# Page tiles laid out on the host for a compressed attention branch, and weights laid out chunk by chunk

## The chip, the cores and the metric

The kernel runs on one core of one Trainium2 chip. The metric is the device time of one launch in microseconds (us), the median of several runs. Laying arrays out anew with numpy before the launch is outside the metric; the arithmetic stays on the chip.

The engines are named as the profile names them: PE is TensorE (PEld its weight loads), DVE is VectorE, ACT is ScalarE, POOL is GpSimd and SP is SyncE, which only issues transfers here.

## The reference

One inference step of a decoder of two layers (width 1024, feed-forward width 2816) over 288 tokens: 256 of a new sequence, and 4 each for 8 running sequences that have 2048 tokens behind them. Each layer is feed-forward, mixer, feed-forward:

```python
for i in range(2):
    x = x + 0.5 * swiglu(rmsnorm(x, norm_ffa[i]), w_ffa_gu[i], w_ffa_down[i])
    h = rmsnorm(x, norm_mix[i])
    x = x + (short_conv_mixer(h) if i == 0 else nsa(h))
    x = x + 0.5 * swiglu(rmsnorm(x, norm_ffb[i]), w_ffb_gu[i], w_ffb_down[i])
y = rmsnorm(x, norm_final)
```

The second mixer is an attention with three branches (compressed, selected, window). The change concerns the compressed branch of the running sequences. Its cache lies in pages of 128 tokens that `page_table` names, 16 pages for each sequence. Every 32 rows of a page become one key and one value:

```python
blk = rows.reshape(B, T // 32, 32, 2, 4, 64) + pe[:, None, None, :]
k = gelu(einsum('bnlkd,lde->bnke', blk[:, :, :, 0], w1k)) @ w2k
v = gelu(einsum('bnlkd,lde->bnke', blk[:, :, :, 1], w1v)) @ w2v
```

Since `pe` is the same for all blocks, the kernel multiplies it by `w1` once and adds the result as a bias `b1`.

## The kernel before, in words

Tokens lie along the free axis: `xT` holds 8 tiles of 128 features by 288 tokens. A product takes a 128x128 piece of weights as the stationary operand. Weights and activations are split in two parts each (`whi`, `wlo`; `xh`, `xl` or `Ah`, `Al`), and three products hi*hi, hi*lo and lo*hi of 288 columns are added up. One unit is such a piece of all 8 feature tiles, 24 products.

Weights come through the class `Weights` (lines 66 to 146). A chunk of up to 1 MB is loaded on SP's queue into one of four `raw` tiles (line 96); it holds two units. `convert` (lines 101 to 123) makes `whi` on ACT (line 116) and `wlo` on DVE or POOL (line 117), two units ahead of the product; when a chunk is used up, the load of the fourth chunk behind it is issued. A chunk is a block of columns of the weight matrix, so each of the 128 partitions reads 8 separate runs of 1 KB (512 bytes in the narrow first chunks).

`begin` (line 329) is the first product of the first layer. It loads `xT` in three parts (line 1454) between the first weight chunks, splits and multiplies as the parts land, and sums the squares. `load_rest` (line 190) sends the convolution state `sT` and the page table `ptb`, the latter to all 128 partitions, on POOL's queue.

In a feed-forward layer (line 431) a gate and an up product give `pg` and `pu`; DVE scales both by `rB`, ACT makes the silu, POOL the gate product `a` (line 456), ACT and DVE split it into `Ah` and `Al`. The 22 pieces go in two halves of 12 and 10, and behind each half comes its part of the down projection. The norm factor `rB` of each stage comes late, from a statistics product `acc<-ss,ones` (line 322).

The compressed branch runs beside all this as a generator, `cmp_side` (line 670). The main program calls `tick` after each unit, and a pacing class lets the generator go on when enough work has passed; `fill.hold` stops it at the end of a stage. Its steps before the change: compute row numbers from the page table on POOL and DVE (`indices`, line 625); load 64 tiles of cached rows with indirect loads on POOL (line 688); turn each on DVE in 32x32 blocks into `rt` (line 694); multiply the bias from `pe` and `W1` on POOL, two long operations (line 707), and reduce it on DVE (line 711); then 16 times a block of 32 small products `acc<-rt,W` over four turned tiles, the second products of the block before (`acc<-Hs,W`, `acc<-W,Hs`), and the gelu on ACT, DVE and POOL (lines 651 to 662), whose result is `Hs`.

Each engine runs its instructions in the order in which the program issues them; the pools of buffers add waits for tiles that are still in use.

Of the kernel before, what the change touches and what calls it, by code (L numbers as in the profile page):

```python
# [10 lines left out]
F32 = mybir.dt.float32  # L11
# [13 lines left out]
NB = 8  # L25
# [13 lines left out]
RAW, SPLIT, RT = 4, 4, 5  # L39
# [25 lines left out]

class Weights:
# [5 lines left out]
    def __init__(self, nc, raw, split, bufs):  # L72
# [8 lines left out]
    def chunk(self, loads, nk, cols):  # L81
        self.chunks.append((loads, nk, cols))
        return len(self.chunks) - 1
# [61 lines left out]
def tile_step(ctx, tc, x_turned, vectors, state_turned, cache_cmp, sel_pages, cache_win, win_pages, page_table,  # L145
              w_ffa_gu, w_ffa_down, w_ffb_gu, w_ffb_down,
              w_conv_in, w_conv_out, w_nsa_in, w_cmp_k1, w_cmp_k2, w_cmp_v1, w_cmp_v2, w_nsa_out,
# [34 lines left out]
    ptb = ffn0.tile([P, P], I32, name="ptb", bufs=1)  # L182
# [27 lines left out]
    W = Weights(nc, raw, split, RAW)  # L210

    def cols_of(w2d, cols, w=256):
        v = w2d.rearrange("(k p) c -> p k c", p=P)
        return [(lambda t: t, v[:, :, cols:cols + w])]
# [4 lines left out]
    def plan_ffn(gu, down, first=False):  # L219
        for f0, f1 in HALVES:  # L220
# [3 lines left out]
            for f, e in zip(cuts, cuts[1:]):  # L224
                g = W.chunk(cols_of(gu, f * P, (e - f) * P), KD, (e - f) * P)
                u = W.chunk(cols_of(gu, FF + f * P, (e - f) * P), KD, (e - f) * P)
# [3 lines left out]
            m = (f1 - f0) // 2  # L230
            dv = down.rearrange("(k p) c -> p k c", p=P)
            for d in range(0, KD, 2):
                cs = [W.chunk([(lambda t: t, dv[:, f0 + i * m:f0 + (i + 1) * m, d * P:d * P + 256])], m, 256)
                      for i in range(2)]
# [4 lines left out]
    def plan_conv():  # L239
        for d in range(0, KD, 2):  # L240
            for part in (1, 2, 0):
                c = W.chunk(cols_of(w_conv_in[0], part * D + d * P), KD, 256)
                for h in range(2):
                    W.unit(c, half(h))
        for d in range(0, KD, 2):
            c = W.chunk(cols_of(w_conv_out[0], d * P), KD, 256)
# [3 lines left out]
    plan_ffn(w_ffa_gu[0], w_ffa_down[0], first=True)  # L250
    plan_conv()
    plan_ffn(w_ffb_gu[0], w_ffb_down[0])
    plan_ffn(w_ffa_gu[1], w_ffa_down[1])

    def plan_nsa():
        v = w_nsa_in[0].rearrange("(k p) c -> p k c", p=P)
        for t in range(6):
            c = W.chunk([(lambda t: t, v[:, :, D + t * 256:D + (t + 1) * 256])], KD, 256)
            for h in range(2):
                W.unit(c, half(h))  # L260
        c = W.chunk([(lambda t: t, v[:, :, D + 6 * 256:N_IN])], KD, 48)
        W.unit(c, lambda v: v)
        for pr in range(2):
            for gp in range(2):
                loads = []
                for kp in range(2):
                    c0 = (2 * pr + kp) * 256 + gp * P
                    loads.append((lambda t, kp=kp: t[:, :, kp * P:(kp + 1) * P], v[:, :, c0:c0 + P]))
                c = W.chunk(loads, KD, 256)
                for gg in range(2):  # L270
                    W.unit(c, lambda v, gg=gg: v.rearrange("p k (kp x) -> p k kp x", kp=2)[:, :, :, gg * HD:(gg + 1) * HD])
        W.attention = len(W.chunks)
        o = w_nsa_out[0].rearrange("(pr kp g d) c -> kp d pr g c", pr=2, kp=2, d=HD)
        for d in range(0, KD, 2):
            loads = []
            for kp in range(2):
                for pr in range(2):
                    loads.append((lambda t, kp=kp, pr=pr: t[kp * HD:(kp + 1) * HD, pr * 4:(pr + 1) * 4],
                                  o[kp, :, pr, :, d * P:d * P + 256]))
            c = W.chunk(loads, KD, 256)  # L280
            for h in range(2):
                W.unit(c, half(h))
        W.stop = W.attention

    plan_nsa()
    plan_ffn(w_ffb_gu[1], w_ffb_down[1])
# [42 lines left out]
    def begin(pg, pu):  # L329
# [26 lines left out]
        sq = []  # L356
        for d in range(0, KD, 3):
            n = min(3, KD - d)
            sq.append(ffn0.tile([P, 3, N], F32, name="rt", bufs=RT)[:, :n])
# [261 lines left out]
    idxc = const.tile([P, 64], I32, name="idxc")  # L621
    pti = const.tile([1, NB * 16], I32, name="pti")
    rows_c = cache_cmp[0].rearrange("n (q l) c k d -> (n q) (l c k d)", l=2)

    def indices():

        pi = ffn0.tile([P, 4], I32, name="pi", bufs=1)
        nc.gpsimd.iota(pi[:, 0:1], pattern=[[0, 1]], base=0, channel_multiplier=1)
        for j, (sh, m) in enumerate(((0, 3), (2, 7), (5, 3))):
            nc.vector.tensor_scalar(pi[:, j + 1:j + 2], pi[:, 0:1], sh, m, op0=OP.logical_shift_right, op1=OP.bitwise_and)  # L630
        pf = ffn0.tile([P, 4], F32, name="pf", bufs=1)
        nc.vector.tensor_copy(pf, pi)
        off = ffn0.tile([P, 4], F32, name="offc", bufs=1)
        nc.vector.scalar_tensor_tensor(off[:, 0:1], pf[:, 1:2], 4.0, pf[:, 3:4], op0=OP.mult, op1=OP.add)
        nc.vector.tensor_scalar(off[:, 0:1], off[:, 0:1], 4.0, None, op0=OP.mult)
        for i in range(1, 4):
            nc.vector.tensor_scalar(off[:, i:i + 1], off[:, 0:1], float(i), None, op0=OP.add)
        pj = ffn0.tile([P, 8], I32, name="pj", bufs=1)
        nc.gpsimd.iota(pj, pattern=[[1, 8]], base=0, channel_multiplier=0)
        hot = ffn0.tile([P, 8], F32, name="hot", bufs=1)  # L640
        nc.vector.tensor_scalar(hot, pj, pf[:, 2:3], None, op0=OP.is_equal)
        pt = ffn0.tile([P, 16, 8], F32, name="pt", bufs=1)
# [874 lines left out]
```

## Time and profile before

| | us |
|---|---|
| median of 3 runs | 1301.99 (1301.74 to 1303.49) |
| profiled execution | 1301.96 |
| its span, first to last instruction | 1300.1 |

| engine | busy us | share | instructions |
|---|---|---|---|
| PE | 1253.6 | 96% | 10679 |
| DVE | 805.6 | 62% | 1476 |
| ACT | 584.1 | 45% | 1050 |
| POOL | 310.0 | 24% | 317 |

The granted TensorE clock is at its full level in nearly all of the span. The transfers move 262 MB, 202 GB/s on average. Products overlap, so that each shows about 0.3 us although one starts every 0.13 us; a busy share of PE therefore tells that no gap was long, not how dense the products are. The stages in order of time: the first feed-forward layer to about 245 us, the convolution mixer to 366, two feed-forward layers to about 826, the projections of the attention to 914, the attention itself to 1050, and the last feed-forward layer.

### The profile page before, as it was taken

Reading aid. Unit: us, or ns where it says so; the run is one execution under the profiler, and the core shown is the slowest. Engines: PE = TensorE matmul, PEld = TensorE weight load, DVE = VectorE, ACT = ScalarE, POOL = GpSimd, SP = SyncE. Lnnn points to the kernel's source line nnn. Section 1 sums busy time; section 2 is a strip of 40 time slices with the busy share of each in tenths; the row PEclk is TensorE's granted clock in tenths of the full one; section 3 lists DMA queues with packets and bytes.
Section 4 is the critical chain, followed back from the end, with each engine's and each line's share of the span. In section 5 each row is a group of like instructions: output and inputs, shape, how many; then the busy total and the mean of one; then the engine's idle time right before and its main releaser. Section 6 shows DMA issues by size and latency. Waiting matters only on the chain.

```text
span 1300.1 us, 26451 instructions
## 1 busy us (share of the span) xinstructions
PE 1253.6 (96%) x10679; PEld 1198.9 (92%) x10679; DVE 805.6 (62%) x1476; ACT 584.1 (45%) x1050; POOL 310.0 (24%) x317
## 2 busy tenths in 40 slices
PE   8999999899999999999999999999888799999997
PEld 8999999899999999999999999999555489999997
DVE  5766666767677656666765455665566456654553
ACT  5443344433444433345433344543566355433444
POOL 1240322343232312232421021220112022210211
PEclk8999999999999999999999999999899999999999
DMA  8866655766557457566754643896697877776432
GB/s 259 213 221 209 195 172 160 223 197 217 169 168 252 158 189 237 176 186 196 228 186 155 195 135 117 234 297 184 217 359 260 256 180 227 266 243 202 147 105 77
DMA packets 220010, 262.12 MB, mean 202 GB/s; under 512 B 16592, under 2 KB 190288, under 8 KB 219760
## 3 DMA queue, kind: packets, MB, share of 16 engines
q1 hardware_dynamic: 201504, 216.03, 52.4%
q0 software_dynamic: 9536, 42.01, 9.9%
q10 hardware_dynamic: 8848, 2.38, 1.0%
q8 instruction: 84, 1.38, 0.4%
q14 instruction: 38, 0.31, 0.1%
HBM read 257.38 MB, written 11.35 MB: 207 GB/s over the span
## 4 chain that ended last, share of the span: by engine, by line
PE 79%; DVE 9%; ACT 4%; DMA 3%; issue 2%; POOL 2%; SPq 0%; ACTq 0%; DVEq 0%; POOLq 0%
PE mm L176 70%; PE acc L176 7%; DVE wlo L117 3%; PE tr L207 2%; ACT whi L116 2%; DMA raw<-in_w_ffa_gu_dram 1%; DVE rt L694 1%; DVE S L1143 1%; DMA raw<-in_sel_pages_dram 1%; POOL rc L688 1%; DVE rB L326 1%; DMA raw<-in_w_ffb_gu_dram 1%; ACT sq L304 0%; ACT L441 0%; DMA wlo<-in_sel_pages_dram 0%
## 5 line engine op out<-in xcount | busy, mean ns | idle before, releaser
L176 PE MATMUL mm<-xh,whi 128*128 128x288 f32 x1832 | 547.4, 299 | 5.6 <-ACT xh L295 3.7
L176 PE MATMUL mm<-xh,wlo 128*128 128x288 f32 x1832 | 543.8, 298 | 1.5 <-DVE wlo L117 1.5
L176 PE MATMUL mm<-xl,whi 128*128 128x288 f32 x1832 | 536.4, 293 | 0.0
L117 DVE TENSOR_TENSOR wlo<-raw,whi 128x1024 fp32r<-128x1024 f32 (+2 forms) x360 | 410.0, 1151 | 116.4 <-ACT whi L116 115.0
L116 ACT ACTIVATE whi<-raw 128x1024 fp32r<-128x1024 f32 (+2 forms) x365 | 343.2, 953 | 90.5 <-PE mm L176 80.9
L176 PEld LDWEIGHTS mm<-xh,whi 128*128 128x128 f32 x1832 | 345.1, 188 | 9.0 <-ACT xh L295 4.4
L176 PEld LDWEIGHTS mm<-xl,whi 128*128 128x128 f32 x1832 | 348.9, 191 | 0.4
L176 PEld LDWEIGHTS mm<-xh,wlo 128*128 128x128 f32 x1832 | 343.9, 188 | 2.5 <-DVE wlo L117 2.4
L176 PE MATMUL mm<-Ah,wlo 128*128 128x288 f32 x768 | 228.8, 298 | 1.6 <-DVE wlo L117 1.6
L176 PE MATMUL mm<-Ah,whi 128*128 128x288 f32 x768 | 228.1, 297 | 0.0
L176 PE MATMUL mm<-Al,whi 128*128 128x288 f32 x768 | 227.2, 296 | 0.0
L456 POOL TENSOR_TENSOR a<-s,t 128x288 f32<-128x288 f32 x88 | 102.3, 1163 | 364.8 <-DVE t L454 238.8
L176 PEld LDWEIGHTS mm<-Ah,wlo 128*128 128x128 f32 x768 | 144.2, 188 | 2.7 <-DVE wlo L117 2.7
L176 PEld LDWEIGHTS mm<-Ah,whi 128*128 128x128 f32 x768 | 144.7, 188 | 0.5
L176 PEld LDWEIGHTS mm<-Al,whi 128*128 128x128 f32 x768 | 144.8, 189 | 0.2 <-DVE Al L535 0.2
L688 POOL DMA_INDIRECT rc<-in_cache_cmp_kv_dram,idxc x64 | 85.9, 1343 | 180.2 <-DVE rt L694 125.5
L452 ACT ACTIVATE s<-t 128x288 f32<-128x288 f32 x88 | 39.1, 445 | 167.0 <-DVE t L450 166.8
L459 ACT ACTIVATE Ah<-a 128x288 fp32r<-128x288 f32 x88 | 39.2, 445 | 115.0 <-POOL a L456 114.7
L454 DVE TENSOR_TENSOR t<-mm,rB 128x288 f32<-128x288 f32 x88 | 40.1, 456 | 78.3 <-PE mm L176 77.6
L694 DVE STREAM_TRANSPOSE rt<-rc 128x1024 f32<-128x1024 f32 x64 | 79.1, 1236 | 0.0
L460 DVE TENSOR_TENSOR Al<-a,Ah 128x288 fp32r<-128x288 f32 x88 | 39.8, 453 | 49.3 <-ACT Ah L459 49.3
L490 DVE SCALAR_TENSOR_TENSOR xT<-mm,xT 128x288 f32<-128x288 f32 x64 | 29.2, 456 | 66.4 <-PE mm L176 66.1
(299 smaller groups left out, 998.2 us busy)
## 6 DMA issues: line engine op xcount, KB each, us to landing
raw<-in_w_ffb_gu_dram SPq DMA_DIRECT2D x44, 1024.0 KB
raw<-in_w_ffa_gu_dram SPq DMA_DIRECT2D x42, 1024.0 KB
early<-in_sel_pages_dram SPq DMA_DIRECT2D x56, 256.0 KB
raw<-in_sel_pages_dram SPq DMA_DIRECT2D x56, 256.0 KB
raw<-in_w_ffa_down_dram SPq DMA_DIRECT2D x16, 768.0 KB
raw<-in_w_conv_in_dram SPq DMA_DIRECT2D x12, 1024.0 KB
raw<-in_w_ffb_down_dram SPq DMA_DIRECT2D x16, 768.0 KB
raw<-in_w_ffa_down_dram SPq DMA_DIRECT2D x16, 640.0 KB
```

Of the source, the lines that this page charges most:

```text
L116: self.nc.scalar.activation(parts[0], v, AF.Copy)
L117: (lower or self.nc.vector).tensor_sub(parts[1], v, parts[0])
L176: nc.tensor.matmul(out, lhsT, rhs, start=start, stop=stop, skip_group_check=True)
L207: nc.tensor.transpose(out, in_, ident[:k, :k])
L452: nc.scalar.activation(s1, t1, AF.Silu)
L454: nc.vector.tensor_mul(t2, pu[:, :N], rB)
L456: nc.gpsimd.tensor_mul(a, s1, t2)
L459: nc.scalar.activation(Ah[:, f], a, AF.Copy)
L460: nc.vector.tensor_sub(Al[:, f], a, Ah[:, f])
L490: nc.vector.scalar_tensor_tensor(xT[:, d], py[:, :N], 0.5, xT[:, d], op0=OP.mult, op1=OP.add)
L688: nc.gpsimd.indirect_dma_start(out=tiles[i], out_offset=None, in_=rows_c, in_offset=bass.IndirectOffsetOnAxis(ap=idxc[:, i:i + 1], axis=0))
L694: nc.vector.transpose(turned[i], tiles.pop(i))
```

## The change

On the host, numpy lays out two things anew. All weights of one chunk lie one behind the other in the order of the chunks, so that each partition reads one run of 4 to 8 KB. The compressed branch's pages lie turned, 128 partitions (half of a token pair and 64 dimensions) by 512 values, as the products need them; `w_cmp1` and `w_cmp2` join key and value weights.

In the kernel, the indices, the indirect loads and the turns go. A tile `cp` holds eight pages, all that one block of products needs. SP reads the numbers of two pages from the page table (`TENSOR_LOAD`) and issues one load of 256 KB for each. A block's moving operand has runs of 16 values in each of eight pages, where it had runs of 32 in four. The bias is summed in short operations on POOL alone. `sT` and the page table are loaded on SP's queue, after the weight loads that `begin` has issued, and the table goes to one partition. The products, their number and their shapes stay.

```diff
     def load_rest():
-        nc.gpsimd.dma_start(sT, state_turned)
-        nc.gpsimd.dma_start(ptb, bass.AP(tensor=page_table.tensor, offset=page_table.offset, ap=[[0, P], [1, P]]))
+        nc.sync.dma_start(sT, state_turned)
+        nc.sync.dma_start(pti, page_table.rearrange("(o b) n -> o (b n)", o=1))
...
-            loads, nk, cols = self.chunks[self.loaded]
+            src, nk, cols = self.chunks[self.loaded]
             t = self.raw.tile([P, 2048], F32, name="raw")
-            v = t[:, :nk * cols].rearrange("p (k c) -> p k c", c=cols)
-            for put, src in loads:
-                self.nc.sync.dma_start(put(v), src)
-            self.tiles[self.loaded] = v
+            self.nc.sync.dma_start(t[:, :nk * cols], src)
+            self.tiles[self.loaded] = t[:, :nk * cols].rearrange("p (k c) -> p k c", c=cols)
...
+    def page_numbers(n, k):
+
+        return nc.values_load_multi_w_load_instructions(
+            pti[0:1, n:n + k], engines=(mybir.EngineType.SP,), min_val=0, max_val=sel_pages.shape[0] - 1,
+            skip_runtime_bounds_check_because="the page table's entries are pages of the caches")[1]
+
     def cmp_side(cw):
...
-        def load(i):
-            if i < 64:
-                tiles[i] = cw.tile([P, 1024], F32, name="rc", bufs=4)
-                nc.gpsimd.indirect_dma_start(out=tiles[i], out_offset=None, in_=rows_c,
-                                             in_offset=bass.IndirectOffsetOnAxis(ap=idxc[:, i:i + 1], axis=0))
-
-        def turn(i):
-            if i < 64:
-                turned[i] = cw.tile([P, 1024], F32, name="rt", bufs=RT)
-                nc.vector.transpose(turned[i], tiles.pop(i))
-                load(i + 4)
...
+        def load(n, j):
+
+            if n < 2 * NB:
+                if j == 0:
+                    tiles[n] = cw.tile([P, 8, 512], F32, name="cp")
+                for k, at_ in enumerate(page_numbers(n * 8 + j * 2, 2)):
+                    nc.sync.dma_start(tiles[n][:, j * 2 + k:j * 2 + k + 1], cmp_pages[bass.ds(at_, 1)].rearrange("s p c -> p s c"))
...
         part = []
         for h in range(2):
-            t = cw.tile([P, 1024], F32, name="rt", bufs=RT).rearrange("p (s e) -> p s e", s=8)
-            nc.gpsimd.tensor_tensor(t, W1[:, 8 * h:8 * h + 8],
-                                    vecT[:, V_PE + 8 * h:V_PE + 8 * h + 8, None].to_broadcast([P, 8, P]), op=OP.mult)
+            t = [cw.tile([P, N], F32, name=x) for x in ("t1", "t2", "s1", "a")]
             part.append(cw.tile([P, P], F32, name="Hx" if h else "Hs"))
+            for q in range(4):
+                v = t[q][:, :256].rearrange("p (s e) -> p s e", s=2)
+                s0 = 8 * h + 2 * q
+                nc.gpsimd.tensor_tensor(v, W1[:, s0:s0 + 2], vecT[:, V_PE + s0:V_PE + s0 + 2, None].to_broadcast([P, 2, P]), op=OP.mult)
+                if q:
+                    nc.gpsimd.tensor_add(t[0][:, :256], t[0][:, :256], t[q][:, :256])
             yield WAITS[3] * FILL
-            nc.vector.tensor_reduce(part[h], t.rearrange("p s e -> p e s"), AX.X, OP.add)
-        nc.vector.tensor_add(part[0], part[0], part[1])
+            nc.gpsimd.tensor_add(part[h], t[0][:, :P], t[0][:, P:256])
+        nc.gpsimd.tensor_add(part[0], part[0], part[1])
...
+        for n in range(2 * NB):
+            H = accb()
+            v = tiles.pop(n).rearrange("p g (c a x) -> p c a g x", c=2, a=16)
+            for st in range(16):
+                for c in range(2):
+                    mm(H[c * 64:(c + 1) * 64, :P], W1[:, st, c * 64:(c + 1) * 64], v[:, c, st], st == 0, st == 15)
...
```

SP's order at the start of the program, before: the weight loads follow one another, each 128 partitions by 8 runs.

```order
L96 DMA raw<-in_w_ffa_gu_dram 128x8x128
L1454 DMA xT<-in_x_turned_dram 128x576 x2
L1454 DMA xT<-in_x_turned_dram 128x1152
L96 DMA raw<-in_w_ffa_gu_dram 128x8x128
L96 DMA raw<-in_w_ffa_gu_dram 128x8x256 x10
L96 DMA raw<-in_w_ffa_gu_dram 128x8x128 x2
L96 DMA raw<-in_w_ffa_down_dram 128x6x256 x8
```

The same place of the changed kernel:

```order
L138 DMA raw<-in_w_ffa_gu_dram 128x1024
L1419 DMA xT<-in_x_turned_dram 128x576 x2
L1419 DMA xT<-in_x_turned_dram 128x1152
L138 DMA raw<-in_w_ffa_gu_dram 128x1024
L138 DMA raw<-in_w_ffa_gu_dram 128x2048 x4
L233 DMA sT<-in_state_turned_dram 128x128
L234 DMA pti<-in_page_table_dram 1x128
L138 DMA raw<-in_w_ffa_gu_dram 128x2048 x5
L649 TENSOR_LOAD pti
L667 ISA
L667 DMA cp<-in_cmp_pages_dram 128x512
```

The state and the table stand behind the sixth weight load, and page loads (with a number load for every two) stand between the later ones.

DVE's order at the start of the convolution mixer, before; `rB` is the norm factor, `t` and `s` are evacuations of products, `rt` a turned tile:

```order
L326 RECIPROCAL rB<-rms 128x288
L549 TENSOR_TENSOR t_2789<-mm,rB 128x288
L655 TENSOR_SCALAR Hs<-Hs 128x128
L694 STREAM_TRANSPOSE rt<-rc 128x1024
L549 TENSOR_TENSOR t_2801<-mm,rB 128x288
L694 STREAM_TRANSPOSE rt<-rc 128x1024
L117 TENSOR_TENSOR wlo<-raw,whi 128x1024
```

And PE's order at the same place of the changed kernel, from the last product before the statistics to the first after the block:

```order
L218 MATMUL mm<-xh,wlo 128x288
L218 MATMUL acc<-ss,ones 128x288
L218 MATMUL acc<-cp,W_509 64x128 x32
L218 MATMUL acc<-Hs,W_77 64x64 x2
L218 MATMUL acc<-W_77,Hs 32x64 x4
L218 MATMUL mm<-xh,whi 128x288
```

The turns are gone from DVE, and the block of 32 small products, which stood 48 products behind the statistics product, now stands directly behind it.

POOL's order around the bias, before (`a` is the gate product, `rc` a tile of rows that is loaded):

```order
L456 TENSOR_TENSOR a<-s_990,t_992 128x288
L456 TENSOR_TENSOR a<-s_1058,t_1060 128x288
L688 DMA rc<-in_cache_cmp_kv_dram,idxc 128x1024
L707 TENSOR_TENSOR rt<-W_537,vecT 128x1024 x2
L688 DMA rc<-in_cache_cmp_kv_dram,idxc 128x1024
```

And in the changed kernel:

```order
L464 TENSOR_TENSOR a<-s_1008,t_1010 128x288
L685 TENSOR_TENSOR Hs<-t_964 128x128
L681 TENSOR_TENSOR t_1075<-W_509,vecT 128x256
L681 TENSOR_TENSOR t_1076<-W_509,vecT 128x256
L683 TENSOR_TENSOR t_1075<-t_1075,t_1076 128x256
L681 TENSOR_TENSOR s_1077<-W_509,vecT 128x256
L683 TENSOR_TENSOR t_1075<-t_1075,s_1077 128x256
L681 TENSOR_TENSOR a<-W_509,vecT 128x256
L683 TENSOR_TENSOR t_1075<-t_1075,a 128x256
L464 TENSOR_TENSOR a<-s_1089,t_1091 128x288
L685 TENSOR_TENSOR Hx<-t_1075 128x128
L686 TENSOR_TENSOR Hs<-Hs,Hx 128x128
```

The bias stood behind the twelfth gate product, the last of the first half; now seven operations stand ahead of the eleventh (an equal block, not shown) and seven ahead of the twelfth.

## Rows read from the trace of the kernel before

**Rows 1.** Stretches: length, busy us of each engine, PEclk granted, DMA share, GB/s.
```profile
390.00:600.00 210.00, 209.81 (x1787) 207.10 (x1786) 130.62 (x182) 87.17 (x142) 55.68 (x55) 1.00 0.61 196
```

**Rows 2.** Timeline of ACT at the start: start, us, operation, idle before and releaser.
```profile
4.86 1.06 ACT L116 ACTIVATE whi<-raw 128x1024 fp32r<-128x1024 f32 x1 [2.14 <-DMA raw<-in_w_ffa_gu_dram]
...
10.12 0.96 ACT L295 ACTIVATE xh<-xT,vecT 128x288 fp32r<-128x288 f32 x2 [3.35 <-DMA xT<-in_x_turned_dram]
11.66 1.81 ACT L295 ACTIVATE xh<-xT,vecT 128x288 fp32r<-128x288 f32 x4 [0.59 <-DMA xT<-in_x_turned_dram]
...
16.41 1.06 ACT L116 ACTIVATE whi<-raw 128x1024 fp32r<-128x1024 f32 x1 [1.14 <-DMA raw<-in_w_ffa_gu_dram]
...
19.42 2.01 ACT L116 ACTIVATE whi<-raw 128x1024 fp32r<-128x1024 f32 x2 [0.56 <-DMA raw<-in_w_ffa_gu_dram]
```

**Rows 3.** Chain of waits, first 30 us: start, us, what.
```profile
21.46 2.35 DVE wlo L117 x2
...
26.39 3.68 PE mm L176 x26
```

**Rows 4.** Stretches of 2 us at the start, columns as in rows 1.
```profile
6.00:8.00 2.00, 1.33 (x4) 0.67 (x4) 2.00 (x3) 0.77 (x2) 0.00 (x0) 1.00 0.84 103
8.00:10.00 2.00, 0.00 (x0) 0.00 (x0) 0.03 (x1) 0.00 (x0) 0.00 (x0) 0.58 0.98 348
```

**Rows 5.** Transfer queues from 4 to 9 us: packets, MB, share of 16 engines.
```profile
q0 software_dynamic: 63, 0.13, 31.0%
```

**Rows 6.** Stretches of 2 us at the mixer's start, columns as in rows 1.
```profile
256.00:258.00 2.00, 0.80 (x10) 0.80 (x12) 2.00 (x3) 0.00 (x0) 0.58 (x1) 0.88 0.12 49
...
262.00:264.00 2.00, 2.00 (x11) 2.00 (x10) 1.58 (x3) 0.39 (x2) 0.26 (x1) 0.50 1.08 389
264.00:266.00 2.00, 2.00 (x16) 2.00 (x16) 1.03 (x1) 1.89 (x2) 0.71 (x1) 0.92 0.39 72
```

**Rows 7.** Timeline of PE at the mixer's start.
```profile
257.20 1.72 PE L176 MATMUL acc<-rt,W 128*64 128x128 f32 x16 [2.55 <-DVE rt L694]
259.77 0.48 PE L176 MATMUL acc<-Hs,W 64*64 64x64 f32 x4 [0.85 <-POOL Hs L662]
```

**Rows 8.** Timeline of PE, inside the mixer and at two layer starts.
```profile
289.02 0.40 PE L176 MATMUL mm<-xh,wlo 128*128 128x288 f32 x1 [0.53 <-DVE wlo L117]
...
387.20 0.27 PE L176 MATMUL acc<-Hs,W 64*64 64x64 f32 x2 [0.64 <-POOL Hs L662]
...
626.87 0.33 PE L176 MATMUL acc<-Hs,W 64*64 64x64 f32 x4 [0.65 <-POOL Hs L662]
```

**Rows 9.** Groups of POOL: operation, count, busy us, mean ns, idle before.
```profile
L508 POOL TENSOR_TENSOR ue<-t,s 128x256 f32<-128x256 f32 x8 | 5.9, 734 | 15.0 <-DVE ue L507 14.8
```

**Rows 10.** Timeline of POOL at the end of the first half.
```profile
78.08 0.81 POOL L456 TENSOR_TENSOR a<-s,t 128x288 f32<-128x288 f32 x1 [0.52 <-DVE t L454]
...
90.76 1.36 POOL L456 TENSOR_TENSOR a<-s,t 128x288 f32<-128x288 f32 x1 [4.76 <-DVE t L454]
...
95.96 3.75 POOL L707 TENSOR_TENSOR rt<-W,vecT 128x1024 f32<-128x1024 f32 x2
```

**Rows 11.** Chain of waits at the same place.
```profile
95.38 5.18 DVE wlo L117
```

**Rows 12.** Timeline of DVE at the same place.
```profile
78.59 1.37 DVE L117 TENSOR_TENSOR wlo<-raw,whi 128x1024 fp32r<-128x1024 f32 x1 [0.69 <-ACT whi L116]
...
84.38 0.96 DVE L117 TENSOR_TENSOR wlo<-raw,whi 128x768 fp32r<-128x768 f32 x1
...
94.17 0.92 DVE L117 TENSOR_TENSOR wlo<-raw,whi 128x768 fp32r<-128x768 f32 x1
```

**Rows 13.** Chain of waits: one block without second products, and a run of products.
```profile
139.13 3.64 PE acc L176 x64
142.77 31.92 PE mm L176 x240
```

**Rows 14.** Line 947, number loads of the attention: ns min/median/max, first and last start.
```profile
L947 SPq TENSOR_LOAD <-pti x32: 297/300/714, 856.0 to 1021.4; - x32
```

**Rows 15.** Waits of SP's queue: us in total, times, longest.
```profile
SPq L96 <- DVE wlo L117: 552.9, 100, 15.8
```

More of the change, by code (lines that the diff above doesn't have):

```diff
@@ L79, in __init__, with chunk @@
         self.stop = None
-    def chunk(self, loads, nk, cols):
-        self.chunks.append((loads, nk, cols))
+    def chunk(self):
+        name, _, steps, cols = next(self.plan)
+        nk, n = len(steps), sum(len(c) for c in cols)
+        at, self.at[name] = self.at[name], self.at[name] + P * nk * n
+        self.chunks.append((self.given[name][at:at + P * nk * n].rearrange("(p n) -> p n", p=P), nk, n))
         return len(self.chunks) - 1
@@ L207, in tr, with plan_ffn @@
         nc.tensor.transpose(out, in_, ident[:k, :k])
[L210 to L214, printed above, removed]
+    W = Weights(nc, raw, split, RAW, dict(
+        w_ffa_gu=w_ffa_gu, w_ffa_down=w_ffa_down, w_ffb_gu=w_ffb_gu, w_ffb_down=w_ffb_down, w_conv_in=w_conv_in,
+        w_conv_out=w_conv_out, w_nsa_in=w_nsa_in, w_nsa_out=w_nsa_out))
     def half(h):
         return lambda v: v[:, :, h * P:(h + 1) * P]
-    def plan_ffn(gu, down, first=False):
+    def plan_ffn(first=False):
         for f0, f1 in HALVES:
@@ L224, in plan_ffn @@
             for f, e in zip(cuts, cuts[1:]):
[L225 to L226 removed]
+                g, u = W.chunk(), W.chunk()
                 for h in range(e - f):
@@ L229, in plan_ffn @@
                     W.unit(u, half(h))
-            m = (f1 - f0) // 2
-            dv = down.rearrange("(k p) c -> p k c", p=P)
             for d in range(0, KD, 2):
-                cs = [W.chunk([(lambda t: t, dv[:, f0 + i * m:f0 + (i + 1) * m, d * P:d * P + 256])], m, 256)
-                      for i in range(2)]
+                cs = [W.chunk(), W.chunk()]
                 for h in range(2):
@@ L237, in plan_ffn, with plan_pairs @@
                         W.unit(c, half(h))
[L239 to L246, printed above, removed]
+    def plan_pairs(n):
+        for _ in range(n):
+            c = W.chunk()
             for h in range(2):
@@ L248, in plan_conv @@
                 W.unit(c, half(h))
[L250 to L283, printed above, removed]
@@ L285, in tile_step @@
-    plan_nsa()
-    plan_ffn(w_ffb_gu[1], w_ffb_down[1])
+    plan_ffn(first=True)
+    plan_pairs(3 * KD // 2 + KD // 2)
+    plan_ffn()
+    plan_ffn()
+    plan_pairs(6)
+    W.unit(W.chunk(), lambda v: v)
+    for _ in range(4):
+        c = W.chunk()
+        for gg in range(2):
+            W.unit(c, lambda v, gg=gg: v.rearrange("p k (kp x) -> p k kp x", kp=2)[:, :, :, gg * HD:(gg + 1) * HD])
+    W.attention = W.stop = len(W.chunks)
+    plan_pairs(KD // 2)
+    plan_ffn()
     xh = const.tile([P, KD, N], F32R, name="xh")
@@ L620, in tile_step @@
     b1 = const.tile([P, 1], F32, name="b1")
[L621 to L642, printed above, removed]
[L643 to L649 removed]
     def gelu_hidden(H, w, pool):
         x, x2 = [pool.tile([P, P], F32, name=n)[:, :w] for n in ("Hx", "Hs")]
[L653 removed]
+        nc.scalar.activation(x if len(H.shape) == 2 else x.rearrange("e (k g n) -> e k g n", k=H.shape[1], g=H.shape[2]), H, AF.Identity, bias=b1)
         nc.scalar.activation(x2, x, AF.Square)
@@ L697, in cmp_side @@
-        for i in range(4):
-            load(i)
-            yield WAITS[2] * FILL
-        for i in range(RT - 2):
-            turn(i)
-            yield WAITS[3] * FILL
+        W1 = load_w1(cw)
+        nc.scalar.dma_start(W2, w_cmp2)
+        yield WAITS[1] * FILL
+        tiles = {}
+        def load(n, j):
[4 more added lines that the diff above has]
+                    nc.sync.dma_start(tiles[n][:, j * 2 + k:j * 2 + k + 1], cmp_pages[bass.ds(at_, 1)].rearrange("s p c -> p s c"))
@@ L717, in cmp_side @@
         yield 0.3
-        turn(RT - 2)
-        yield 0.3
-        turn(RT - 1)
         def second_of(Hs, b, h):
@@ L945, in load_chunk @@
             if j != "w":
-                n = b * 16 + j * 4
-                _, at_ = nc.values_load_multi_w_load_instructions(
-                    pti[0:1, n:n + 4], engines=(mybir.EngineType.SP,), min_val=0, max_val=sel_pages.shape[0] - 1,
-                    skip_runtime_bounds_check_because="the page table's entries are pages of the cache")
+                at_ = page_numbers(b * 16 + j * 4, 4)
             s0 = 0
```

119 lines of the change are left out of this document (68 added, 51 removed).

## The prediction

> **What bounds the kernel now.** I read the page first, then the stretches, then the waits of each engine in the stretches that are not full. The page has TensorE busy nearly throughout, and the stretches show where the little that is left lies: inside the feed-forward layers TensorE is busy 209.81 of 210 us at full clock [rows 1]. There VectorE, GpSimd and the transfers can win nothing, however much is taken off them: the 64 turns of compressed rows that vanish keep VectorE busy, but next to none of them was waited for. So I look only at places where TensorE waits and the change touches what it waits for: the first 26 us, the start of the convolution mixer, the two layer starts behind it, and the end of the first half of the first feed-forward layer. The attention stage idles most, but its pages, order and operations stay, so I count it as nothing, with 1.5 us either way for its transfers.
>
> **A. The start.** Before, ScalarE begins the first weight split at 4.86, then sits idle 3.35 and 0.59 us for the two later parts of `xT`, and 1.14 and 0.56 us for the third and fourth weight loads; the fourth split starts at 19.42 [rows 2]. Behind it the chain is fixed: two splits on ScalarE, 2.35 us of `wlo`, then `rB`, and TensorE enters its steady run at 26.39 [rows 3]. From 4.86 to 19.42 the queue brought `xT` (1.18 MB) and three weight chunks (0.52, 1.05, 1.05 MB): 3.8 MB in 14.56 us, 261 GB/s. The hole is at 6 to 8 us, 103 GB/s against 348 in the next stretch [rows 4], and GpSimd's queue is what stands in it: 0.13 MB took 31.0% of the 16 engines' time for 5 us [rows 5]. These are the convolution state and the page table sent to 128 partitions. After the change SyncE issues both behind the sixth weight load, and the table goes to one partition. At 348 GB/s the 3.8 MB take 10.9 us and the fourth split starts at 15.8, 3.6 us earlier. ScalarE does not prevent it: of the 14.56 us it idled 5.64, so its own work is 8.9 us. The chunk layout also makes the runs longer (512 bytes and 1 KB become 4 and 8 KB); the best rate of the rows used here is 389 GB/s [rows 6], which would give 4.8. I take -4.0, nearest to the 348, with bounds -1 (the chain behind the split is held by something else) and -6 (389 GB/s and an earlier first chunk).
>
> **B. The start of the convolution mixer.** Before, TensorE stops in the middle of a block of compressed rows: 2.55 us for a VectorE turn that stands behind `rB` and two evacuations, then 0.85 us for `Hs` on GpSimd, itself queued behind an indirect load [rows 7]. The granted clock then falls to its lower level: 0.88 on average in one 2 us stretch, 0.50 in the three after it, 0.92 in the last [rows 6], that is 0.48 + 6.00 + 0.32 = 6.8 us at 1.2 GHz. Less the 0.85 idle in it, 6.0 us of work ran at half speed, 3.0 us lost. In the new order the block stands right behind the statistics product, its page tile was loaded long before, no turn exists, and the `Hs` it needs is put between the square sums. The block (3.64) and two more products (6.4 us of TensorE) then cover `rB`. All goes: -2.55 - 0.85 - 3.0 = -6.4, with bounds -2.5 (another wait follows and the clock still falls) and -6.7.
>
> **C. Smaller waits.** TensorE waits 0.64 and 0.65 us for `Hs` at two layer starts and 0.53 us for a `wlo` behind a turn inside the convolution [rows 8]. The first two had `Hs` behind an indirect load; in the new order it is made before the evacuations. -1.3 and -0.5, bounds 0 and -2.5 together.
>
> **D. What the change adds on GpSimd.** The sums for the bias `b1` were two long multiplications on GpSimd and two reductions on VectorE; now they are 17 short GpSimd operations. They fall behind the tenth and eleventh gate product of the first half, just before the twelfth, whose result the down projection needs at once. A 256-wide operation takes 0.73 us alone [rows 9]. From the tenth gate product's end (78.89) two blocks of seven (5.1 each), two gate products (0.81 each) and a sum (taken as 0.5) end at 91.2, before the 92.12 at which the twelfth gate product ended before [rows 10]: cost 0. But VectorE does not run freely beside GpSimd here: the chain of waits has one `wlo`, whose usual time at this shape is 0.92 to 0.96, lasting 5.18 us from 95.38 [rows 11, 12], while the two long bias multiplications run from 95.96 to 99.71 [rows 10]. One waits for the other. Between 78.59 and 95.09 VectorE has six `wlo` and three `Al` [rows 12], all with two SBUF inputs, together 7.7 us. If some 5.7 of this comes between the GpSimd operations, the twelfth gate product ends at 96.9 and `Ah` at 97.3. TensorE gets to it at about 94.5 (its last up product ends some 0.6 before the 90.76 at which that gate product started, then 33 products of 0.133 [rows 13]): 2.8 us of wait, and 0.8 for a late `wlo`, less about 0.8 that the old multiplications cost at the same place. +3.0, bounds 0 and +6 (VectorE shut out through a whole block, or the lower clock behind the stall). The Trainium skill (SBUF — State Buffer, section "SBUF: two separate sides") says that GpSimd and a VectorE operation with two SBUF inputs share one port pair, which the first to start holds for its whole instruction while the other blocks entirely. By that rule, with which the trace's 5.18 us agree, the short blocks cost the +3; without it they would cost nothing and the sum would end 3 us lower.
>
> **E. What is hidden.** The blocks on TensorE keep their count of 16 and their 64 records each, 3.64 us [rows 13]. SyncE gets 64 number loads of 0.30 us [rows 14], 19 us in all, and 128 page loads, and waited 552.9 us for weight tiles of one kind alone [rows 15]. Each page load of a later tile waits for the block that frees it, and the next weight loads stand behind it; but those run four chunks, eight products of 3.2 us, ahead, so that SyncE must be held over about 16 us per block before TensorE sees it. Gone at no gain: 64 indirect loads, the turns, and nine small weight loads on ScalarE's queue.
>
> **Sum.** -4.0 - 6.4 - 1.3 - 0.5 + 3.0 = -9.2 us. The profiled execution took 1301.96 us (1300.1 in the span, 1.86 around it), beside a median of 1301.99, so the two need no correction: 1292.8 us.
>
> **Rivals.**
> The bias blocks cost nothing, because GpSimd slips between VectorE's operations. For it: most gate products in the trace are not stretched; against it, the 5.18 us above. A to C whole, D at 0: 1289.8, and with 389 GB/s at the start 1289.0.
> Half the gain: the clock falls once more, behind D or in the start, and a late split takes the place of the turn at the mixer. For it: the stall of 2.55 us had 6.8 us of the lower clock behind it [rows 6, 7]. D at +6 and B at -5: 1297.2.
> No change: the start is bound by ScalarE and VectorE after all, and something new waits at the mixer. Against it, the 5.64 us that ScalarE spent waiting for transfers. A at -1, B at -2.5, C at 0, D at +3: 1301.5.
> Slower: TensorE reads the pages in runs of 16 elements, 2 KB apart, where it read runs of 32. The place is the 16 blocks; if the shorter run slows the reading twofold, each costs 3.64 us more, 58 in all, less 9.2: 1351. It decides from 0.6 us per block, 16%. Against it: at runs of 32 a record of 128 columns takes 57 ns, as fast per column as a plain product of 288 at 0.133 us [rows 13], so runs do not show yet. No row has pages in runs of 16.
>
> **How the numbers follow.** Within 0.2% (2.6 us, 1299.4 to 1304.6) a measurement of this kernel cannot be told from no change. Forecast 0.52 (1290.5 to 1295.5), no bias cost 0.24, half 0.11, no change 0.08, slower 0.05. The first three are faster: 0.87; same 0.08; slower 0.05. For eight in ten I take the first two whole, down to 1286.5 where A and C reach their bounds, and the half case to its upper side, 1298.5.
>
> **What would show it.** A: the fourth split starts at 15 to 16 us, no stretch near 103 GB/s between 4 and 14, the steady run enters at 22 to 23. B: no TensorE wait over 0.5 us in the first mixer products, granted clock 1.00 there. C: the two waits for `Hs` gone. D: a TensorE wait of 2 to 4 us in the first down projection, `wlo` of 2 us and more beside the short bias operations. E: blocks of 3.6 to 3.8 us, SyncE still waiting for weight tiles. The forecast fails if a block is over 4.3 us, if page tiles make TensorE wait, or if D grows past 6 us.

## The result and the profile after

| | before | changed |
|---|---|---|
| median, us | 1302.19 (4 runs, 1301.74 to 1303.49) | 1291.82 (4 runs, 1289.71 to 1292.10) |
| ratio | | 0.9915 (95% interval 0.990 to 0.993) |
| profiled execution, its span | 1301.96, 1300.1 | 1289.71, 1288.0 |

The forecast was 1292.8. The profiled execution of the changed kernel is the fastest of its four, so its trace shows a gain of 12.2 us where the medians show 10.4. On another chip, beside 21 runs of the kernel before, the changed kernel took 1291.05 (e4 below).

The head of the page after; the columns are engine, busy us, share and instructions:

```profile
PE 1249.7 (97%) x10679; PEld 1193.7 (93%) x10679; DVE 724.8 (56%) x1394; ACT 583.6 (45%) x1050; POOL 251.1 (19%) x264
```

VectorE lost 81 us and GpSimd 59 us of work. That by itself is not where the 10 us come from: TensorE has as many instructions as before, and the time is gained where it waits less.

To place the gain, the start of the same instruction is read in both traces: the first gate product on GpSimd, the last update of `xT` of a layer on VectorE, and so on, at points where both kernels have run the same number of blocks.

| stage | to this instruction | before, us | after, us | gain in the stage | forecast |
|---|---|---|---|---|---|
| start | first gate product | 26.80 | 22.27 | -4.5 | -4.0 |
| first feed-forward layer | its last `xT` | 238.73 | 235.19 | +1.0 | +3.0 |
| mixer and start of the next layer | an `xT` of the next layer | 586.64 | 577.48 | -5.6 | -6.4 - 0.5 - 0.6 |
| rest up to the attention | last `xT` | 834.43 | 824.58 | -0.7 | -0.7 |
| attention | next gate product | 1086.60 | 1074.13 | -2.6 | 0 |

A second trace of the changed kernel (e4) has the same gains within 0.1 us in the four stages ahead of the attention, and -2.3 in the attention. The start is less steady from trace to trace: its mark lay between 21.68 and 23.02 in the variants of the changed kernel, none of which touches it.

Start, ScalarE of the changed kernel (start us, us, operation, idle before and releaser):

```profile
4.57 1.06 ACT L158 ACTIVATE whi<-raw 128x1024 fp32r<-128x1024 f32 x1 [1.89 <-DMA raw<-in_w_ffa_gu_dram]
...
8.10 1.81 ACT L302 ACTIVATE xh<-xT,vecT 128x288 fp32r<-128x288 f32 x4 [0.76 <-DMA xT<-in_x_turned_dram]
...
11.88 1.06 ACT L158 ACTIVATE whi<-raw 128x1024 fp32r<-128x1024 f32 x1 [0.20 <-DMA raw<-in_w_ffa_gu_dram]
...
14.37 2.02 ACT L158 ACTIVATE whi<-raw 128x1024 fp32r<-128x1024 f32 x2
```

The waits of [rows 2], 5.64 us, have shrunk to 0.96, and the fourth split starts 5.05 us earlier. The stretches (columns as in [rows 1]) show no hole any more, and more than the 348 GB/s of [rows 4]:

```profile
6.00:8.00 2.00, 1.97 (x11) 1.43 (x10) 2.00 (x4) 1.34 (x4) 0.00 (x0) 1.00 1.03 422
8.00:10.00 2.00, 2.00 (x16) 1.80 (x15) 1.94 (x6) 1.90 (x5) 0.00 (x0) 1.00 1.05 442
```

In the chain of waits TensorE enters its steady run at 21.86 (26.39 in [rows 3]):

```profile
21.86 8.18 PE mm L218 x60
```

The bias, on GpSimd and then on TensorE (timelines):

```profile
80.04 1.33 POOL L681 TENSOR_TENSOR a<-W,vecT 128x256 f32<-128x256 f32 x1
...
84.82 1.34 POOL L683 TENSOR_TENSOR t<-t,t 128x256 f32<-128x256 f32 x1
86.11 0.61 POOL L681 TENSOR_TENSOR s<-W,vecT 128x256 f32<-128x256 f32 x1
86.80 0.74 POOL L683 TENSOR_TENSOR t<-t,s 128x256 f32<-128x256 f32 x1
87.50 1.33 POOL L681 TENSOR_TENSOR a<-W,vecT 128x256 f32<-128x256 f32 x1
88.91 0.73 POOL L683 TENSOR_TENSOR t<-t,a 128x256 f32<-128x256 f32 x1
89.60 0.79 POOL L464 TENSOR_TENSOR a<-s,t 128x288 f32<-128x288 f32 x1
```

```profile
90.92 0.40 PE L218 MATMUL mm<-Ah,whi 128*128 128x288 f32 x1 [0.95 <-ACT Ah L467]
91.71 0.40 PE L218 MATMUL mm<-Al,whi 128*128 128x288 f32 x1 [0.39 <-DVE Al L468]
```

The twelfth gate product stands at the end of a row of seven operations; the down projection waits 0.95 us for its `Ah` and 0.39 for its `Al`.

The start of the mixer: the chain of waits of [rows 7]'s place is now TensorE alone, and the clock is full in every stretch of the mixer's start, as in this one (0.50 at the same place in [rows 6]):

```profile
239.92 1.58 PE mm L218 x12
241.50 4.95 PE acc L218 x78
246.45 15.67 PE mm L218 x117
```

```profile
244.00:246.00 2.00, 2.00 (x37) 1.76 (x34) 0.97 (x2) 0.04 (x1) 0.00 (x0) 1.00 0.92 363
```

A block without second products takes what it took in [rows 13], so runs of 16 values cost nothing (chain of waits):

```profile
109.25 3.64 PE acc L218 x64
```

Something new stands at the end of the mixer: the first two of these three waits on TensorE's timeline.

```profile
349.09 0.40 PE L218 MATMUL mm<-Ah,whi 128*128 128x288 f32 x1 [0.55 <-ACT whi L158]
350.35 0.40 PE L218 MATMUL mm<-Ah,wlo 128*128 128x288 f32 x1 [0.73 <-DVE wlo L159]
357.31 0.40 PE L218 MATMUL mm<-xh,wlo 128*128 128x288 f32 x1 [0.73 <-DVE wlo L159]
```

The third stood in the kernel before as well, at the same product, and there it was the only one:

```profile
365.76 0.40 PE L176 MATMUL mm<-xh,wlo 128*128 128x288 f32 x1 [0.73 <-DVE wlo L117]
```

What ScalarE of the changed kernel does there:

```profile
343.00 1.04 ACT L158 ACTIVATE whi<-raw 128x1024 fp32r<-128x1024 f32 x1
345.70 0.54 ACT L302 ACTIVATE xh<-xT,vecT 128x288 fp32r<-128x288 f32 x1 [1.66 <-DVE xT L573]
346.15 0.43 ACT L311 ACTIVATE sq<-xT 128x288 f32<-128x288 f32 x1
346.59 1.28 ACT L449 ACT_TABLE_LOAD   x1
347.89 0.20 ACT L449 ACTIVATE root<-eps 128x1 f32<-128x1 f32 x1
348.00 1.04 ACT L158 ACTIVATE whi<-raw 128x1024 fp32r<-128x1024 f32 x1
```

From 339.62 to 357.31 the chain of waits runs through `whi`, `wlo`, `xT` and `sq` and not through TensorE: the splits set the pace, 3.48 us for most output tiles. The chain of the kernel before runs through the same splits from 344 us on, at the same pace and with the same table load for the square root (line 449 here; 354.92 before). But there TensorE had run a block until 342, during which the splits went on, and their lead over it lasted until the wait at 365.76. In the new order the last block of the mixer ends at 306, and the lead is used up by 349.

What this costs shows when the same product of TensorE, with as many blocks ahead of it, is read in both traces. The changed kernel is ahead by 3.5 us at the mixer's first product (234.99 against 238.53), by 10.8 in the out projection (338.43 against 349.26), and by 8.4 at the statistics product behind it (361.12 against 369.57). So the mixer gains 7.3 us and then loses 2.4 again; with the 0.6 us of a wait for `Hs` behind it, that is the -5.6 of the table.

### The profile page after: what moved, and what is told of

It reads as the page before. It is cut to its first block, busy times and chain, and to the rows that moved or that the text cites. A ratio compares the mean times of both kernels' runs of the same rounds, so it can differ in the third digit from the quotient of the medians.

```text
span 1288.0 us, 26738 instructions
## 1 busy us (share of the span) xinstructions
PE 1249.7 (97%) x10679; PEld 1193.7 (93%) x10679; DVE 724.8 (56%) x1394; ACT 583.6 (45%) x1050; POOL 251.1 (19%) x264
## 4 chain that ended last, share of the span: by engine, by line
PE 85%; DVE 5%; ACT 4%; issue 2%; POOL 1%; SPq 1%; DMA 1%; ACTq 0%; DVEq 0%; POOLq 0%
PE mm L218 75%; PE acc L218 9%; PE tr L249 2%; DVE wlo L159 2%; ACT whi L158 1%; SPq L922 1%; DVE S L1108 1%; ACT sq L311 1%; ACT L449 0%; POOL t L683 0%; POOL a L464 0%; DMA raw<-in_sel_pages_dram 0%; ACT S L1109 0%; DMA wlo<-in_sel_pages_dram 0%; DVE PA L1141 0%
## 5 line engine op out<-in xcount | busy, mean ns | idle before, releaser
L159 DVE TENSOR_TENSOR wlo<-raw,whi 128x1024 fp32r<-128x1024 f32 (+2 forms) x360 | 405.0, 1138 | 120.1 <-ACT whi L158 118.8
L464 POOL TENSOR_TENSOR a<-s,t 128x288 f32<-128x288 f32 x88 | 114.9, 1305 | 492.9 <-DVE t L462 318.4
L218 PE MATMUL acc<-cp,W 128*64 128x128 f32 x1024 | 59.4, 274 | 0.0
L218 PEld LDWEIGHTS acc<-cp,W 128*64 128x64 f32 x1024 | 55.6, 137 | 2.8 <-issue 2.8
```

The costliest lines, as they stand in the source:

```text
L159: (lower or self.nc.vector).tensor_sub(parts[1], v, parts[0])
L218: nc.tensor.matmul(out, lhsT, rhs, start=start, stop=stop, skip_group_check=True)
L464: nc.gpsimd.tensor_mul(a, s1, t2)
```

## The experiments

Each time is a median; the edits are against the kernel that the text names. "Marks" are the instructions of the table above.

**The start: two edits, each alone.**

```diff
 # e1, the kernel before
-        nc.gpsimd.dma_start(sT, state_turned)
-        nc.gpsimd.dma_start(ptb, bass.AP(...))
+        nc.sync.dma_start(sT, state_turned)
+        nc.sync.dma_start(ptb, bass.AP(...))
```

> The kernel before with one edit: the convolution state and the page table (still to 128 partitions) go on SyncE's queue behind the sixth weight load instead of GpSimd's queue at the program's start. Theory (POOL's packets are the hole at the start): the 103 GB/s stretch at 6 to 8 us goes, the fourth split starts near 16 us instead of 19.42, the first gate product on POOL near 23 instead of 26.80, time 1298 to 1299. Rival (the chunk layout makes the start faster): hole and start stay, 1301.5 to 1302.5.

```diff
 # e2, the kernel before, with weight_chunks and its host arrays of the changed kernel
-            for put, src in loads:
-                self.nc.sync.dma_start(put(v), src)
+            self.nc.sync.dma_start(t[:, :nk * cols], src)
```

> The kernel before with one edit: the weights lie chunk by chunk, so that each partition reads one run; state and page table stay on GpSimd's queue, indirect loads and turns stay. Theory (POOL's packets are the hole): the stretch at 6 to 8 us stays far below its neighbours, the first gate product on POOL comes at 25 or later (before 26.80, changed kernel 22.27), time 1300.5 to 1302. Rival (the layout carries the start): first gate product at 22 to 23, time 1297.5 to 1298.5. If both edits are needed, neither run reaches 22.3.

e1 took 1299.38 (ratio 0.998, 0.997 to 0.999), e2 1300.11 (0.998, 0.997 to 0.999). The first gate product came at 23.74 and 24.02, 3.1 and 2.8 us earlier than before; both edits together give 4.5. The stretch from 6 to 8 us, e1 and then e2:

```profile
6.00:8.00 2.00, 1.83 (x7) 1.10 (x7) 2.00 (x4) 1.54 (x4) 0.00 (x0) 1.00 1.00 351
```

```profile
6.00:8.00 2.00, 1.41 (x6) 0.99 (x7) 1.89 (x3) 1.80 (x5) 0.00 (x0) 1.00 1.02 183
```

e1 came close to its theory; e2 fell between its two. The two transfers on GpSimd's queue make the hole: where they are moved it is gone (e1, 351), and where they stay it stays (e2, 183). Whether their queue or their moment does it is open, since e1 changes both. The layout has a share of its own that both theories left out: it lifts the other stretches, from 348 to 418 and more. Neither theory was right alone, and the shares overlap, since 3.1 + 2.8 is more than 4.5.

Both runs keep the turns and the indirect loads, and both still stop at the mixer's start: 2.55 and 2.57 us for a turn, 1.48 us each for `Hs`. So neither of these two edits is what removes that stop.

**The bias.**

```diff
 # e3, the changed kernel: the 17 operations are left out, and the product of their sum
+        nc.vector.memset(b1, 0.0)
```

> The changed kernel without the 17 short bias operations on GpSimd; the bias is set to zero, so this part of the computation is left out, and the steps of the generator keep their places. Theory by the trace of the changed kernel: the two waits of TensorE at 89.7 and 90.9 us (0.95 and 0.39 us) go and nothing else, 1.0 to 1.6 us less than the changed kernel: about 1290.5. The prediction's term: 3.0 less, 1288.8. Rival (GpSimd slips between VectorE's operations): no change, 1291.8.

```diff
 # e5, the changed kernel: two operations behind each of the first eight page loads, and no rows of seven
         for n in range(2):
             for j in range(4):
                 load(n, j)
+                bias(4 * n + j)      # one product, one sum
                 yield WAITS[2] * FILL
```

> The changed kernel with the same bias sums, but two GpSimd operations at a time, one pair beside each of the eight first page loads (between the third and the tenth gate product) instead of seven ahead of the eleventh and seven ahead of the twelfth; the blocks on TensorE stay where they are. Theory (a row of seven operations delays the twelfth gate product, on which the down projection waits): no wait of TensorE at 89.7 and 90.9 us, about 2 us less than the changed kernel, 1289.2. Rival (GpSimd's operations cost VectorE's splits their port wherever they stand): waits for wlo in the middle of the half, 1291 or more.

e3 took 1290.64 and e5 1289.54 beside 1291.05 and 1291.82 of the changed kernel. By the marks the gain within the first layer is larger than e3's time tells: from the first gate product to the last `xT`, 212.92 us in the changed kernel, 210.88 in e3, 211.05 in e5. So the row of bias operations cost 1.9 to 2.0 us and, spread in pairs, next to nothing. e3's time hides it because in its trace the start came 0.75 us later and the attention stage was 1.8 us longer than in the changed kernel's trace (see e4). In e5 TensorE has no idle at the place (columns as before: TensorE first, busy 12.00 of 12):

```profile
80.00:92.00 12.00, 12.00 (x92) 12.00 (x91) 6.74 (x11) 5.12 (x8) 2.58 (x2) 1.00 0.44 139
```

**The same kernel again.** e4 is the changed kernel, unedited.

> The changed kernel as it is, on the same chip as its variants. Time 1291.8. What it is to tell apart is the attention stage, which ended 2.6 us earlier in the first trace of the changed kernel than in that of before. If that gain belongs to the change, this trace shows it too (from the last evacuation of the fourth feed-forward half to the first gate product of the last layer: 249.6 us, against 252.2 before). If it is the chance of the page loads' landing, this one lies between 249.6 and 252.2 or above.

1291.05. Its attention stage took 249.9 us, as in the first trace (249.6). The variants with the same attention were less even: e7 252.1, e5 251.8, e3 251.4, the others 250.1 to 250.8. The kernel before took 252.2, and e1 and e2, which keep its attention, 253.0 and 252.2. So the ten traces of the new attention, 250.7 on average, all lie below the three of the old one, 252.4 on average, if at the edge only by 0.1. Some 1.7 us may belong to the change; no run isolates a cause, and the rest is spread from trace to trace. A long stage and a short one, e3 and e4, differ in two things. One is TensorE's waits for page loads, on its timeline in e3 and then in e4 (the kernel before has two as well, the changed one one):

```profile
1012.27 0.62 PE L218 MATMUL mm<-raw,Qbd 128*32 128x512 f32 x2 [1.06 <-DMA raw<-in_sel_pages_dram]
1017.60 0.62 PE L218 MATMUL mm<-raw,Qbd 128*32 128x512 f32 x2 [0.90 <-DMA raw<-in_sel_pages_dram]
```

```profile
1018.00 0.62 PE L218 MATMUL mm<-raw,Qbd 128*32 128x512 f32 x2 [0.93 <-DMA raw<-in_sel_pages_dram]
```

The other is the granted clock near the end of the stage, 0.72 on average in e3 and 1.00 in e4:

```profile
1026.00:1032.00 6.00, 4.56 (x26) 3.72 (x28) 4.15 (x19) 2.95 (x11) 0.73 (x1) 0.72 0.87 351
```

```profile
1026.00:1032.00 6.00, 3.87 (x32) 2.67 (x32) 4.59 (x20) 3.01 (x13) 0.80 (x1) 1.00 0.92 370
```

A fall to the lower clock late in the stage stands in every trace of 251.4 us and more; two waits stand in shorter ones too (e6, e9). Why the one falls into the low clock there and the other does not stays open; the instructions ahead of it in the attention are the same.

**The mixer: the place of the block, the turns, the hold.**

```diff
 # e8, the changed kernel: the hold ends 48 products later
                     nc.scalar.activation(root, eps, AF.Silu)
-                    fill.hold = False
...
+                    if d0 == 0 and part == 2 and d == 1:
+                        fill.hold = False
                     tick(3.0)
```

> The changed kernel with the block at the start of the convolution mixer 48 products behind the statistics product, where it stood in the kernel before, and not directly behind it; its pages and Hs come as in the changed kernel. Theory (the wait there was that for the turn, and the place is worth little): no wait over 0.5 us, full clock, 1291 to 1292. Rival (the place does it, since the block covers the norm factor rB): TensorE waits 1 to 3 us for a bank that the evacuation behind rB frees, the clock may fall with it, 1293 to 1296.

```diff
 # e7, the changed kernel: 64 turns back, into a tile that nobody reads
+                turn(n + 1, j)    # nc.vector.transpose(scratch, two pages of the next tile)
                 load(n + 2, j)
```

> The changed kernel with 64 turns of 128x1024 on VectorE put back, one per step of the compressed branch, into a scratch tile that nobody reads; added work, no product waits for it. Theory (the turns cost only where TensorE waited for one): 0 to 1 us more than the changed kernel, 1291.4 to 1292.4. Rival (VectorE's 79 us of turns slowed the splits and evacuations everywhere): 2 us and more, 1293.5 or above, with waits for wlo in many units.

e8 took 1291.20, the same as the changed kernel, with no wait at the mixer's start: the place is worth nothing, and the rival of e8 is out. e7 took 1294.77, 3 to 4 us more, where I expected at most 1. By the marks the turns cost 3.0 us up to the mixer's last `xT` and 4.1 up to the attention, though no product reads what they write. VectorE at the largest wait, and TensorE behind it:

```profile
258.96 1.24 DVE L664 STREAM_TRANSPOSE rt<-cp 128x1024 f32<-128x1024 f32 x1
260.12 0.18 DVE L639 TENSOR_SCALAR Hs<-Hs 128x128 f32<-128x128 f32 x1
260.22 1.22 DVE L159 TENSOR_TENSOR wlo<-raw,whi 128x1024 fp32r<-128x1024 f32 x1
```

```profile
261.49 0.40 PE L218 MATMUL mm<-xh,wlo 128*128 128x288 f32 x1 [1.57 <-DVE wlo L159]
```

The turn stands ahead of a `wlo`, and the wait is `wlo`'s. So turns cost something even where no product reads them. This is not the stop of [rows 7]: e7 has neither the wait for a turn nor the lower clock at the mixer's start, so its 3 us say what turns would cost in the new order, and not how the gain over the kernel before divides.

```diff
 # e6, the changed kernel: in the mixer's out projection alone
-        fill.hold = d >= 3
+        fill.hold = d >= (5 if mixer else 3)
```

> The changed kernel; in the out projection of the convolution mixer the compressed branch is held from the sixth output tile on and not from the fourth, so that one block of 32 small products stands between two of its products (behind the fifth) and not behind the mixer; nothing else moves. Theory (the splits run out of their lead over TensorE there, and the activation table load at the fifth output tile then shows through; a block gives the splits 4.7 us to catch up): the waits of 0.7, 0.89 and 0.89 us of the changed kernel between 348 and 357 us go, about 1.3 to 2 us less, 1289.5 to 1290. Rival (the block only shifts the waits): 1291.4, with the same waits at another place, or a wait for rB at the start of the next layer.

e6 took 1287.73 (ratio 0.989, 0.988 to 0.991). The three waits that were to go are 0.55, 0.73 and 0.73 us on the timeline above. By the marks e6 gains 3.5 us, more than expected; the chain of waits at the place is TensorE alone, with the block (76 records with its second products) in it:

```profile
337.95 3.87 PE mm L218 x29
341.82 4.47 PE acc L218 x76
346.29 16.15 PE mm L218 x120
```

Beside the three waits, 2.0 us, the slower pace of the splits goes: in the changed kernel each output tile took 3.48 us there (`wlo` at 352.55 and 356.03), where 24 products of 0.133 us take 3.2.

**Both edits.**

> The changed kernel with both edits that gained: the bias sums spread beside the first eight page loads, and the hold of the compressed branch from the sixth output tile of the mixer on. Theory (two waits at two places that have nothing to do with each other, -1.9 and -3.5 us by the marks of the traces): 1286 to 1287. Rival (one only uncovers what the other hid): 1287.7 or more.

1285.08 (ratio 0.9875, 0.986 to 0.989): faster than both kernels, 17 us below before. By the marks the start differs by 0.3, the first layer gains 1.8, the mixer 3.5; the two edits add up.

```diff
 # e10, as e9 with the bias on TensorE (its hold too)
+        for s in range(16):
+            mm(pb[:, 0:1], W1[:, s], vecT[:, V_PE + s:V_PE + s + 1], s == 0, s == 15)
```

> As the run with both edits, but the bias sums are 16 products of one column on TensorE, and GpSimd has none of them. Theory (spread in pairs, GpSimd's operations cost nothing any more): 0.5 to 2 us slower than the run with both edits, by what the 16 weight loads take on TensorE. Rival (GpSimd's pairs still cost VectorE's splits): as fast or faster than it.

1291.79, 6.7 more than e9, far over the 0.5 to 2 expected. TensorE's timeline and the stretches:

```profile
104.01 4.85 PE L218 MATMUL acc<-vecT,W 128*128 128x1 f32 x32
```

```profile
104.00:106.00 2.00, 2.00 (x21) 2.00 (x19) 0.46 (x1) 0.84 (x1) 0.00 (x0) 1.00 0.00 0
106.00:108.00 2.00, 2.00 (x12) 2.00 (x11) 0.00 (x0) 0.00 (x0) 0.00 (x0) 0.54 0.00 0
108.00:110.00 2.00, 2.00 (x10) 2.00 (x10) 1.10 (x3) 0.00 (x0) 0.00 (x0) 0.50 0.00 0
```

The 16 one-column products (32 records) take 4.85 us, and the granted clock falls to its lower level in the midst of them and stays there for the products behind; by the marks the first layer is 6.4 us longer than in e9. So e10's time does not tell whether GpSimd's pairs still cost something. The first layer of e5 beside that of e3 does: 211.05 against 210.88, at most 0.2 us.

**SyncE and the transfers.**

```diff
 # e11, the changed kernel
                     nc.sync.dma_start(tiles[n][:, ...], cmp_pages[bass.ds(at_, 1)]...)
+                    nc.sync.dma_start(again[:, ...], cmp_pages[bass.ds(at_, 1)]...)
```

> The changed kernel with each of the 128 page loads issued twice, the second into a scratch tile that nobody reads: 33.6 MB and 128 DMA issues more on SyncE's queue, nothing else. Theory (SyncE and the transfers have slack over the weight loads, which run four chunks ahead): 0 to 1 us more than the changed kernel, 1291.4 to 1292.5. Rival (the queue is close to its end, and weight loads come late behind page loads): 1294 and more, with ScalarE's splits waiting for raw tiles.

1291.19: no difference. SyncE, with 128 more issues, still waited 586.4 us for one kind of weight tile (waits of its queue; 624.4 in the changed kernel, 552.9 in [rows 15]):

```profile
SPq L138 <- DVE wlo L159: 586.4, 121, 13.7
```

## Why the prediction was right, point by point

The time lay 1.0 us under the forecast, inside its own range. That the sum came out so well is in part luck: in the trace the bias cost 2.0 less than forecast, the stage of the mixer gained 1.9 less, and the attention gained 2.6 that the working had put at nothing.

**A, the start (-4.0, measured -4.5).** Right in place and size: the fourth split at 14.37 where 15 to 16 was forecast, the steady run at 21.86 (22 to 23). The step "at 348 GB/s the 3.8 MB take 10.9 us" took its rate from a stretch with the old layout; with the new one the queue brought 406 to 442 GB/s from 4 to 18 us. e1 and e2 show the two causes.

**B and the `wlo` of C (-6.4 - 0.5).** Right as to the waits: none of them is left, the clock is full, and up to the out projection TensorE gains 7.3 us, where these terms add up to 6.9. "No turn exists" was the step that carried it, as far as the runs tell: e1 and e2 keep turns and indirect loads and keep the stop, and e8 shows that the block's place is worth nothing. Turns and indirect loads were not taken out one without the other. That the block covers `rB` was true and not needed. The stage as a whole gained only 5.6, and here "all goes" failed: the waits were counted at the mixer's start, and what the moved blocks take away from its end was not. In the new order no block stands between 306 us and the mixer's end, and 2.4 us are lost there; e6 wins back 3.5.

**C, the waits for `Hs` (-1.3).** Both are gone.

**D, the bias (+3.0, measured +1.0 against before).** The mechanism and the place were right, the size was not. By the same product of TensorE, the changed kernel is ahead by 4.5 us at the first product of the down projection (85.41 against 89.94), by 2.7 behind its two waits (93.68 against 96.33), and by 3.5 once the kernel before has had its own wait there (100.08 against 103.62). So the old multiplications cost 0.9, where the working had 0.8, and the new operations 1.9, where it had 2.8 and 0.8. (Its three terms add up to 2.8 and not 3.0.) "Some 5.7 of this comes between" was too large: four of the 14 long operations met VectorE and lasted 1.33 to 1.76 instead of 0.61 to 0.74, 3.1 us together. So the twelfth gate product began at 89.60 and not some 2 us later, and TensorE waited 1.3 us, not 2.8. The Trainium skill (SBUF — State Buffer, section "SBUF: two separate sides") has the first of the two hold the shared ports for its whole instruction; the trace agrees in kind: the operation begun at 80.04, inside a `wlo` of VectorE from 79.77 to 80.91, lasted 1.33. The 5.18 us of [rows 11] fit it less well than the working says, since there the `wlo`, begun at 95.38, was the first of the two, ahead of the multiplications at 95.96, and was still the one that lasted. GpSimd's indirect load from 94.52 to 95.94 may have been the first; no run shows it. What the rule can't say is how often the two meet, and that set the price.

**E, what is hidden.** Blocks of 3.64 us and SyncE's slack held (e11). "Next to none of them was waited for" was true of the kernel before and misled: put back in the new order, the turns cost 3 to 4 us (e7). An operation that nobody waits for can still be ahead of one that somebody does.

**Attention (0 within 1.5, measured -2.6).** Outside that margin in both traces of the changed kernel; over all traces the new attention is some 1.7 us shorter. That "its pages, order and operations stay" was the reason to put it at nothing, and it did not hold within the margin; no run here names the cause.

Of the rivals, "slower" fell with the first block of 3.64 us, "no change" with the start, and that the bias blocks cost nothing with e3 and e5. "Half the gain" had named a late split in place of the turn at the mixer: that did happen, 100 us further on, and cost 2.4 us where the rival had 1.4.

## What to carry to other kernels

Filler work between long products is not only a cost: it is where the producers of the next operands catch up. Who moves it must check, from the splits' lead over the products, what comes due in the stretch that it leaves, such as an activation table load. A row of short operations on an engine that also makes an operand on the path is better cut into pairs and put beside earlier work; and an operation that no product waits for still has a price where it stands ahead of others on an engine that runs in order, as the turns of e7 did.

## What the runs showed of the hardware

- With one run of 4 to 8 KB per partition the transfers brought 402 GB/s on average from 2 to 18 us; e1, with runs of 512 bytes and 1 KB, brought 341 in the same stretch. e2, which changes the layout alone, brought 411 to 440 outside its hole.
- TensorE's granted clock fell to its lower level while the engine was counted busy without a gap, during 16 products of one column (e10). Every other fall in the traces of this case came behind idle time, as at 256 to 258 us in the kernel before (0.88 [rows 6]), behind the stop of 2.55 us.
- The attention stage, with the same instructions, took 249.6 to 252.1 us in ten traces of the changed kernel and its variants. A gain under 3 us in another stage must be read at marks within that stage, not off the total.
